# Expert results added to the residual in memory by the store; POOL's branches, its order and the zeroing moved

## The chip, the core and the metric

The kernel runs on one core of a Trainium2 chip. The metric is device microseconds of one execution. A core has a matrix engine (PE), a vector engine (DVE), an activation engine (ACT), a general engine (POOL, which also issues the indirect DMAs and writes their descriptors in software) and a queue engine (SP) that issues plain DMAs. All DMAs share 16 DMA engines. Times below are microseconds (us) from the start of the profiled span.

## What is computed

One layer of a diffusion backbone on 512 tokens of width 1024: a token mixer (state-space scan and convolution), then a mixture of 32 experts in 4 groups of 8. Every token chooses one group, and in it two experts. The part that the change touches:

```python
def hier_moe(h, w_rg, b_rg, w_rx, b_rx, w_gate, w_up, w_down):
    group_prob = softmax(h @ w_rg + b_rg)
    p_group, g_idx = top_k(group_prob, 1)
    top_logits, top_idx = top_k(in_group, 2)             # logits of the chosen group's 8 experts
    weights = softmax(top_logits) * p_group
    expert_id = g_idx * 8 + top_idx
    gate = sum(one_hot(expert_id, 32) * weights)
    for e in range(32):
        act = silu(h @ w_gate[e]) * (h @ w_up[e])        # 1024 -> 256
        out = out + gate[:, e:e + 1] * (act @ w_down[e]) # 256 -> 1024
...
x = x + gt2 * hier_moe(modulate(rmsnorm(x, g_ffn), sh2, sc2))
return rmsnorm(x, g_final)
```

Both experts of a token lie in one group, so experts of different groups never share a token. An expert's three weight matrices are 1 MB each, 3 MB together in float32.

## The kernel before

**Up to the experts.** The mixer takes the first 500 us or so. While its last product runs, `route(i)` (L1160) normalises one block of 128 tokens, stores it to the DRAM buffer `h2d`, and finds the block's two experts per token and each token's rank within its expert. The residual rows go to the DRAM buffer `x1d` (L1238). `indices` (L1279) then makes the table `ix` on DVE: for expert and slot, the token's row, twice over, as the first or the second choice of the token; empty slots get an index out of bounds, whose row the DMA leaves alone. `ixh` is the same for half rows.

**Preparation.** POOL zeroes five tiles (`xgs`, three of them, and `xws`, two, 128 x 1024 each) with memsets at L1260. `gather_e(e)` (L1423) fetches up to 64 token rows of an expert from `h2d` into half of an `xgs` tile: POOL loads the expert's size class from `size`, branches over four sizes and issues one indirect DMA of the chosen number of rows. `gather_w(e)` fetches rows 64 to 127 into `xws`, under a branch that is taken only for experts with more than 64 tokens (four experts are such here).

**The loop** at L1731 has 33 passes, step e for e = 0 to 32. The experts' order ORD is the 28 that aren't the last of their group, group by group, and then the four last ones of the groups (DIR), "expert e" being the e-th in this order. In step e PE runs gate and up of expert e (`tile_gu`, L1366: 8 slices of the inner dimension, two column halves each), then four small transposes of expert e-1's activated product (`tile_at`, tiles `sge`, `pat`, `at`; the two copies to `at` are on ACT and DVE), in odd steps the transposes (`turn`) of the next two experts' tokens, and down of expert e-1 (`tile_down`). `second` holds, under branches on PE, the same work for an expert's rows above 64. DVE then scales the result by gt2 into `ye` (`tile_y`), and POOL scatters it with indirect DMAs to `ybuf`, a DRAM buffer of 1024 rows, one for each token and choice (`scatter_e`; the second half again under a branch on size). The weights stream through 20 buffers of 1 MB: `load_p` of SP issues three loads at the end of each step, each as its buffer comes free; the last is number 95. PE, ACT and DVE follow the written order inside the loop (`MAN`, L1703); POOL and SP follow the framework's scheduler.

**ybuf** is zeroed early: POOL fills a tile, and four stores of 1 MB on ACT's queue (`y_zero`, 71 to 92 us) write it out.

**The end.** For tokens without an expert in DIR: SP loads x1 (`last_loads`) and both results of each token (`last_rows`, tile `yr`, after all scatters), ACT and DVE weight and add them (`last_scale`, `last_mix`), POOL adds the sum to x1 with a tensor operation (helper line L98), ACT sums squares (`last_sum`), and after `roots` and `recip` DVE scales (`last_out`) and POOL stores the rows. For tokens with an expert in DIR, the four last experts' rows are finished in place: POOL gathers x1's rows (`own_rows`, tile `ownb`), the token's weights from a small table (`lw` from `pwd`) and its other expert's result from `ybuf` (`own_other`, tile `owny`); DVE adds that (`own_base`) and the expert's own result (`own_sum`), and `own_out` stores the row. The routing weights come from `weights()` (L1266) and `last_tables()` (L1567), both called in step 1.

Where a wait is written with `<-`, the profile names the work that ended last before it; `PEq` is PE's own sequencer working through branches.

Of the kernel before, what the change touches and what calls it, by code (L numbers as in the profile page):

```python
# [26 lines left out]
def hybrid_kernel(  # L27
# [565 lines left out]

    ybuf = dram.tile([2 * L, D], F32, name="ybuf")
    zero = s5m.tile([64, TC, 128], F32, tag="ys", name="zero", bufs=1).rearrange("p t n -> p (t n)")
    G.memset(zero, 0.0)

    def y_zero(j):
        S.dma_start(out=ybuf.rearrange("(p a) d -> p a d", p=64)[:, 4 * j:4 * j + 4], in_=zero.unsqueeze(1).to_broadcast([64, 4, D]))

    MANM = {mybir.EngineType.PE, mybir.EngineType.Activation}
    with tc.manual_schedule(engines=MANM):
# [8 lines left out]
        for j in range(4):  # L611
            KO[f"y{j}"] = lambda j=j: y_zero(j)
# [12 lines left out]
        for o in (  # L625
# [7 lines left out]
        ).split():  # L633
            if o not in done:
                KO[o]()
                done.add(o)
# [327 lines left out]
    G.iota(posf[:, :, :, 1], pattern=[[1, NT], [NT, 2]], base=0, channel_multiplier=0, allow_small_or_imprecise_dtypes=True)  # L964
# [63 lines left out]
    ORD = [x_ for x_ in range(NE) if x_ not in DIR] + list(DIR)  # L1028
# [250 lines left out]
    def indices(pt, p, n, name):  # L1279

        em = mz2.tile([128, 2, n], F32, tag="ixe", name=name + "_e", bufs=1)[0:p]
        t = mz2.tile([128, 2, n], F32, tag="ixs", name=name + "_s", bufs=1)[0:p]
        V.tensor_copy(t, pt)
        V.tensor_scalar(em[:, 0], t[:, 0], 0.0, BIG, op0=ALU.is_equal, op1=ALU.mult)
        V.scalar_tensor_tensor(em[:, 1], t[:, 1], 128.0, t[:, 0], op0=ALU.mult, op1=ALU.add)
        V.scalar_tensor_tensor(em[:, 1], em[:, 0], -1.0, em[:, 1], op0=ALU.add, op1=ALU.add)
        ix = mz2.tile([p, 2, n], I32, tag="ix" + name, name=name)
        V.tensor_copy(ix[:, 1], em[:, 1])
        V.tensor_scalar(em[:, 0], em[:, 1], float(L), -float(L), op0=ALU.is_ge, op1=ALU.mult)
        V.tensor_tensor(ix[:, 0], em[:, 0], em[:, 1], op=ALU.add)  # L1290
        if name == "tb":

            pq = ps_tp("pixh")
            for a in range(2):
                for c in range(2):
                    T.matmul(pq[64 * c:64 * c + 64, n * a:n * a + n], lhsT=ident[:, 64 * a:64 * a + 64], rhs=em[:, 1], start=True, stop=True, skip_group_check=True)
            V.tensor_scalar(ixh.rearrange("p a e -> p (a e)"), pq[:, 0:2 * n], 2.0, cofs, op0=ALU.mult, op1=ALU.add)
        return ix

# [10 lines left out]
    V.tensor_copy(ixw, ix[64:128, 0])  # L1310
# [22 lines left out]
    V.tensor_scalar(s0[:, 1:1 + NE - ND].rearrange("p (g e) -> p g e", g=NGR), c64[:, :, 0:EPG - 1], 64.0, None, op0=ALU.is_gt)  # L1333
    V.tensor_scalar(s0[:, 1 + NE - ND:1 + NE], c64[:, :, EPG - 1], 64.0, None, op0=ALU.is_gt)
# [11 lines left out]
    def scatter(idx, y):  # L1346
        return G.indirect_dma_start(out=ybuf, out_offset=bass.IndirectOffsetOnAxis(ap=idx, axis=0), in_=y, in_offset=None,
                             bounds_check=2 * L - 1, oob_is_err=False)
# [17 lines left out]
    def tile_gu(pg, e, r, a):  # L1366
        st = (xws[e // 2 % 2] if a else xgs[e // 2 % 3]).rearrange("p (k s) -> p k s", k=KD)
        for k in range(KD):
# [29 lines left out]
    def tile_y(pd):  # L1398
# [8 lines left out]
    more = {}  # L1407

    def by_size(e, f, lo=0, hi=len(SIZES)):
        if hi - lo == 1:  # L1410
            return [f(SIZES[lo])]
        mid = (lo + hi) // 2
        with tc.If(more[e] > mid - 1) as big:
            r = by_size(e, f, mid, hi)
        with big.Else():
            r += by_size(e, f, lo, mid)
        return r
# [5 lines left out]
    def gather_e(e):  # L1423

        if e < NE:
            more[e] = load_size(e, EN.Pool)
            p0 = 64 * (e % 2)
            by_size(e, lambda n: gather(xgs[e // 2 % 3][p0:p0 + n], ix[0:n, 0, ORD[e]:ORD[e] + 1]), 0, SIZES.index(64) + 1)

    def gather_w(e):  # L1430

        if e < NE:
            p0 = 64 * (e % 2)
            with tc.If(more[e] > SIZES.index(64)):  # L1434
                gather(xws[e // 2 % 2][p0:p0 + 64], ixw[0:64, ORD[e]:ORD[e] + 1])

    scattered = []

    def scatter_h(e, a, y):
        return G.indirect_dma_start(out=ybuf.rearrange("r (c n) -> (r c) n", c=2), out_offset=bass.IndirectOffsetOnAxis(ap=ixh[:, a, ORD[e]:ORD[e] + 1], axis=0),  # L1440
                                    in_=y[:, 512 * a:512 * a + 512], in_offset=None, bounds_check=4 * L - 1, oob_is_err=False)

    def halves(size_, f):

        r = [f(0)]
        with tc.If(size_ > SIZES.index(64)):  # L1446
            r.append(f(1))
        return r

    def scatter_e(e, y):  # L1450
        ins = halves(more[e], lambda a: scatter_h(e, a, y))

        for i_ in ins:
            for p_ in scattered:
                tc.declare_no_dep(i_.ins if hasattr(i_, "ins") else i_, p_.ins if hasattr(p_, "ins") else p_, reason="rows of different experts")
        scattered.extend(ins)

    for e in range(4):
        gather_e(e)
    for e in range(3):  # L1460
        gather_w(e)
# [4 lines left out]
    with tc.If(n_gen > 0):  # L1466
        with tc.For_i(0, n_gen, 1):
# [17 lines left out]
            for i in range(NT):  # L1485
                for q in range(2):
# [5 lines left out]
                    rg = mz2.tile([128, 2], BF16, tag="rg", name="rg", bufs=2)  # L1492
                    V.tensor_scalar(rg, pos[:, i, q, :], g8[:, 0:1], None, op0=ALU.mult)
                    T.matmul(pt[:, 0:2], lhsT=og, rhs=rg, start=(n == 0), stop=(n == 2 * NT - 1))
                    n += 1
            ixg = indices(pt[:, 0:2].unsqueeze(2), 128, 1, "tg")
# [15 lines left out]
            gather(xg, ixg[:, 0])  # L1512
# [27 lines left out]
            for h in range(2):  # L1540
                V.tensor_tensor(yg[:, 512 * h:512 * h + 512], pd[h], gt2[:, 512 * h:512 * h + 512], op=ALU.mult)
            scattered.append(scatter(ixg[:, 1], yg))
# [4 lines left out]
    x1s, yrs, ids = [], [], {}  # L1547
# [3 lines left out]
    BC = (0, 1, 6, 7)  # L1551
    DC = (2, 4, 8, 10)

    def ins_of(i):
        return i.ins if hasattr(i, "ins") else i

    def after_all(ld):
        for p_ in scattered:
            tc.add_manual_dep(ins_of(ld), ins_of(p_).name, mybir.DependencyInfo(mybir.DependencyClass.Sync, mybir.DependencyReason.DATA), reason="results of every expert")

    def half_rows(t):
# [273 lines left out]
```

## Time and profile before

| | us |
|---|---|
| median of 3 runs | 904.88 (902.15 to 905.14) |
| the profiled execution, its own time | 905.64 |
| its span, first to last instruction | 903.9 |
| PE busy | 708.6 (78%) |
| DVE busy | 497.3 (55%) |
| POOL busy | 370.2 (41%) |
| ACT busy | 321.4 (36%) |
| DMA moved | 202.80 MB, mean 224 GB/s |
| mean granted TensorE clock | 0.91 of full speed |

The shares are means over stages with different limits. The experts' part lies between about 536 us and the end; the rows below are of that part, but for the software queue's, which is of the whole span. In a row of the timeline, the time in square brackets is how long the engine had been idle before the instruction, and what ended that.

### The profile page before, as it was taken

Reading aid. Unit: us, or ns where it says so; the run is one execution under the profiler, and the core shown is the slowest. Engines: PE = TensorE matmul, PEld = TensorE weight load, DVE = VectorE, ACT = ScalarE, POOL = GpSimd, SP = SyncE. Lnnn points to the kernel's source line nnn. Section 1 sums busy time; section 2 is a strip of 40 time slices with the busy share of each in tenths; the row PEclk is TensorE's granted clock in tenths of the full one; section 3 lists DMA queues with packets and bytes.
Section 4 is the critical chain, followed back from the end, with each engine's and each line's share of the span. In section 5 each row is a group of like instructions: output and inputs, shape, how many; then the busy total and the mean of one; then the engine's idle time right before and its main releaser. Section 6 shows DMA issues by size and latency. Waiting matters only on the chain. (4 is left out here: it accounts for less than half of the span.)

```text
span 903.9 us, 14338 instructions
## 1 busy us (share of the span) xinstructions
PE 708.6 (78%) x5334; PEld 484.4 (54%) x5334; DVE 497.3 (55%) x824; ACT 321.4 (36%) x564; POOL 370.2 (41%) x323
## 2 busy tenths in 40 slices
PE   3598967998969977889999963887988999994430
PEld 0476854666657765646788742454555455552200
DVE  4948573365489878538883584332233443430783
ACT  4443512346455747538432311311111121210350
POOL 4656434435386796613400232143132222344342
PEclk9998987999999998989999985897999999998655
DMA  8925951242246464667857385999999999998001
GB/s 308 256 77 161 234 177 53 72 123 71 66 135 193 147 184 139 194 207 287 309 199 274 117 309 167 378 353 344 331 384 367 384 382 380 384 398 323 18 38 56
DMA packets 87160, 202.80 MB, mean 224 GB/s; under 512 B 15025, under 2 KB 44787, under 8 KB 77346
## 3 DMA queue, kind: packets, MB, share of 16 engines
q1 hardware_dynamic: 77410, 177.92, 56.5%
q0 software_dynamic: 7680, 15.30, 5.0%
q10 hardware_dynamic: 1984, 8.44, 3.5%
q8 instruction: 54, 0.88, 0.4%
q14 instruction: 32, 0.26, 0.1%
HBM read 183.05 MB, written 27.23 MB: 233 GB/s over the span
## 5 line engine op out<-in xcount | busy, mean ns | idle before, releaser
L1370 PE MATMUL peg<-eraw,xg 128*64 128x256 f32 x1024 | 120.0, 386 | 8.8 <-PEq L1708 6.9
L1370 PEld LDWEIGHTS peg<-eraw,xg 128*64 128x64 f32 x1024 | 81.3, 139 | 54.7 <-issue 28.7
L1392 PE MATMUL ped<-eraw,at 128*64 128x512 f32 x288 | 77.4, 666 | 18.4 <-ACT at L1385 15.5
L396 PE MATMUL zp<-hh,zuwh 128*128 128x512 f32 x192 | 78.5, 409 | 0.0
L1440 POOL DMA_INDIRECT ybuf<-ye,ixh x31 | 31.2, 1007 | 113.0 <-DVE ye L1402 76.6
L398 PE MATMUL zp<-hh,zuwl 128*128 128x512 f32 x192 | 76.9, 400 | 0.3 <-POOL zuwl L757 0.2
L397 PE MATMUL zp<-hl,zuwh 128*128 128x512 f32 x192 | 76.6, 399 | 0.0
L98 POOL TENSOR_TENSOR adacc<-adacc,wa 128x512 f32<-128x512 f32 x30 | 46.6, 1553 | 42.5 <-ACT wa L857 40.1
L1402 DVE TENSOR_TENSOR ye<-ped,gt2h 128x512 f32<-128x512 f32 x56 | 36.3, 687 | 34.3 <-PE ped L1392 31.8
L1343 POOL DMA_INDIRECT xg<-h2d,tb x32 | 30.0, 937 | 57.0 <-ACT at L1385 33.0
L1385 ACT ACTIVATE at<-pat 128x128 f32<-128x128 f32 x32 | 8.8, 276 | 109.4 <-PE pat L1383 57.5
L1392 PEld LDWEIGHTS ped<-eraw,at 128*64 128x64 f32 x288 | 19.1, 147 | 50.2 <-issue 23.8
L396 PEld LDWEIGHTS zp<-hh,zuwh 128*128 128x128 f32 x192 | 37.2, 194 | 11.8 <-issue 4.4
L1383 PE MATMUL pat<-ident,sge 64*128 64x64 f32 x128 | 16.2, 309 | 34.2 <-DVE sge L1377 34.2
L398 PEld LDWEIGHTS zp<-hh,zuwl 128*128 128x128 f32 x192 | 37.0, 193 | 9.6 <-POOL zuwl L757 1.6
L1386 DVE COPY at<-pat 128x128 f32<-128x128 f32 x32 | 9.3, 292 | 59.0 <-PE pat L1383 48.9
L397 PEld LDWEIGHTS zp<-hl,zuwh 128*128 128x128 f32 x192 | 37.1, 193 | 7.3
L1359 DVE COPY xw<-pxt 128x512 f32<-128x512 f32 x16 | 11.1, 692 | 51.8 <-PE pxt L1354 34.8
L1383 PEld LDWEIGHTS pat<-ident,sge 64*128 64x128 f32 x128 | 11.0, 202 | 48.8 <-DVE sge L1377 36.7
L1377 DVE TENSOR_TENSOR sge<-peg,sge 64x256 f32<-64x256 f32 x64 | 27.4, 428 | 14.5 <-ACT sge L1375 12.7
L98 POOL TENSOR_TENSOR vb<-vta,vtb 128x512 f32<-128x512 f32 x16 | 21.9, 1370 | 30.8 <-PE pv L533 20.0
L1375 ACT ACTIVATE sge<-peg 64x512 f32<-64x512 f32 x32 | 18.9, 590 | 39.9 <-PEq L1708 28.5
(510 smaller groups left out, 1770.1 us busy)
## 6 DMA issues: line engine op xcount, KB each, us to landing
eraw<-in_w_exp_gate_dram SPq DMA_DIRECT2D x24, 1024.0 KB
eraw<-in_w_exp_up_dram SPq DMA_DIRECT2D x24, 1024.0 KB
eraw<-in_w_exp_down_dram SPq DMA_DIRECT2D x24, 1024.0 KB
wa<-in_w_ada_dram SPq DMA_DIRECT2D x32, 512.0 KB
zr<-in_w_in_dram SPq DMA_DIRECT2D x12, 1024.0 KB
wa<-in_w_ada_dram SPq DMA_DIRECT2D x8, 1024.0 KB
eraw<-in_w_exp_gate_dram SPq DMA_DIRECT2D x14, 512.0 KB
eraw<-in_w_exp_down_dram SPq DMA_DIRECT2D x14, 512.0 KB
```

The lines of the kernel that those rows point to most:

```text
L98: G.tensor_tensor(o, a, b, op=op)
L396: T.matmul(acc, lhsT=wh, rhs=ah, start=start, stop=False)
L397: T.matmul(acc, lhsT=wh, rhs=al, start=False, stop=False)
L398: T.matmul(acc, lhsT=wl, rhs=ah, start=False, stop=stop)
L1343: G.indirect_dma_start(out=xg, out_offset=None, in_=h2d, in_offset=bass.IndirectOffsetOnAxis(ap=idx, axis=0), bounds_check=L - 1, oob_is_e ...
L1370: T.matmul(pg[H[c], 256 * a:256 * a + 256], lhsT=st[:, k, H[e % 2]], rhs=r[c][k // 4][:, 256 * (k % 4):256 * (k % 4) + 256], start=(k == 0 ...
L1375: S.activation(sg[64:128], pg[0:64], AF.Silu)
L1377: V.tensor_tensor(sg[H[k], k:512:2], pg[64:128, k:512:2], sg[64:128, k:512:2], op=ALU.mult)
L1383: T.transpose(pas[k][:, 64 * a:64 * a + 64], sg[H[k], 256 * a + k:256 * a + 256:2], ident[H[k], H[k]])
L1392: T.matmul(pd[a][H[c]], lhsT=at[:, 128 * k + 64 * a:128 * k + 64 * a + 64], rhs=r[2][k][:, 512 * c:512 * c + 512], start=(k == 0), stop=(k ...
L1402: V.tensor_tensor(y[:, 512 * a:512 * a + 512], pd[a], gt2h, op=ALU.mult)
L1440: return G.indirect_dma_start(out=ybuf.rearrange("r (c n) -> (r c) n", c=2), out_offset=bass.IndirectOffsetOnAxis(ap=ixh[:, a, ORD[e]:ORD[ ...
```

## The change

- A result is weighted when it leaves PSUM: `slot_weights()`, new and called before the loop, brings each token's routing weight into the order of the expert's slots (`wh`, by matmuls with the one-hot matrix `oh`, in three bfloat16 parts), and `tile_y` multiplies by `wh` and gt2 in one DVE operation.
- `add_e` replaces `scatter_e`: two indirect DMAs per expert (both halves, always) that add the rows to `x1d` in memory (`compute_op=ALU.add`). `ybuf`, its zeroing, `pwd` and `last_tables` are gone. Adds of experts of one group wait for that group's earlier adds; those of other groups share no token and are declared independent.
- ORD takes the groups in turn: expert 0 of each group, then expert 1 of each, and so on. The last four are the same as before.
- POOL follows the written order in the loop, and `gather_e`, `gather_w`, the adds and the final stores are issued always, with no size load and no branch; the gather has always 64 rows.
- The zeroing of `xgs`, `xws`, the PSUM tiles and `ownb` is done by ACT (a copy with scale 0).
- `tile_gu` is split: 6 of 8 slices, then `tile_at`, then the last 2. The first `turn` of `xws` moves behind gu of expert 0.
- The end loads x1 with SP after all adds (`last_rows`, step 28), gathers `ownb` for group j after that group's adds (`own_rows`, one in each of steps 26 to 29), and has no mixing; `last_sum` runs in step 30, the first `roots` and `last_out` in step 31, the rest in step 32 and after it.

The diff, cut to its core:

```diff
-    def y_zero(j):
-        S.dma_start(out=ybuf.rearrange("(p a) d -> p a d", p=64)[:, 4 * j:4 * j + 4], in_=zero.unsqueeze(1).to_broadcast([64, 4, D]))
...
-    ORD = [x_ for x_ in range(NE) if x_ not in DIR] + list(DIR)
+    ORD = [EPG * g_ + i_ for i_ in range(EPG) for g_ in range(NGR)]
...
+    def zero(t):
+        n = t.shape[1] // 128
+        S.activation(t.rearrange("p (k n) -> p k n", k=n), ident.unsqueeze(1).to_broadcast([128, n, 128]), AF.Copy, scale=0.0)
+
     for a_ in xgs + xws:
-        G.memset(a_, 0.0)
+        zero(a_)
...
+    def add_rows(dst, idx, y, rows):
+        return G.indirect_dma_start(out=dst, out_offset=bass.IndirectOffsetOnAxis(ap=idx, axis=0), in_=y, in_offset=None,
+                                    bounds_check=rows - 1, oob_is_err=False, compute_op=ALU.add)
...
-            V.tensor_tensor(y[:, 512 * a:512 * a + 512], pd[a], gt2h, op=ALU.mult)
+            V.scalar_tensor_tensor(y[:, 512 * a:512 * a + 512], pd[a], wh[:, a, ORD[e]:ORD[e] + 1], gt2h, op0=ALU.mult, op1=ALU.mult)
...
     def gather_e(e):
         if e < NE:
-            more[e] = load_size(e, EN.Pool)
             p0 = 64 * (e % 2)
-            by_size(e, lambda n: gather(xgs[e // 2 % 3][p0:p0 + n], ix[0:n, 0, ORD[e]:ORD[e] + 1]), 0, SIZES.index(64) + 1)
+            gather(xgs[e // 2 % 3][p0:p0 + 64], ix[0:64, ORD[e]:ORD[e] + 1])
...
+    def add_e(e, y):
+        added[e] = [add_rows(half_rows(x1d), ixh[:, a, ORD[e]:ORD[e] + 1], y[:, 512 * a:512 * a + 512], 2 * L) for a in range(2)]
+        for n_, i_ in enumerate(added[e]):
+            for e_ in added:
+                for p_ in added[e_][:n_] if e_ == e else added[e_]:
+                    if e_ == e or ORD[e_] // EPG != ORD[e] // EPG:
+                        tc.declare_no_dep(ins_of(i_), ins_of(p_), reason="rows of different tokens")
+                    else:
+                        after(i_, [p_])
+
+    for f, e in ((gather_e, 0), (gather_e, 1), (gather_w, 0), (gather_w, 1), (gather_e, 2), (gather_e, 3), (gather_w, 2)):
+        f(e)
+    weights()
+    slot_weights()
...
     def own_rows(j):
-        own_get(half_rows(x1d), own["b"][j], 1, j, 2 * L)
-        own_get(pwd, own["w"][:, j], 0, j, 4 * L)
+        for a in range(2):
+            ld = G.indirect_dma_start(out=own["b"][j][:, a], out_offset=None, in_=half_rows(x1d),
+                                      in_offset=bass.IndirectOffsetOnAxis(ap=ixh[:, a, DIR[j]:DIR[j] + 1], axis=0), bounds_check=2 * L - 1, oob_is_err=False)
+            after(ld, further + [p_ for e in range(j, NE - ND, NGR) for p_ in added[e]])
...
     def last_rows():
-        for i in range(NT):
-            t = eraw("yr").rearrange("p (q d) -> p q d", q=2)
...
+        for h in range(2):
+            t = eraw("x1").rearrange("p (i d) -> p i d", i=2)
+            ld = SY.dma_start(out=t, in_=x1d[256 * h:256 * h + 256].rearrange("(i p) d -> p i d", p=128))
+            after(ld, further + [p_ for e in added for p_ in added[e]])
+            x1s.extend([t[:, 0], t[:, 1]])
...
-    MAN = {EN.PE, EN.Activation, EN.DVE}
+    MAN = {EN.PE, EN.Activation, EN.DVE, EN.Pool}
...
         for e in range(NE + 1):
+            n_ = e - 1 - NE + ND
             gather_e(e + 4)
             if e > 0:
                 sg = tile_act(pgs[(e - 1) % 2])
+            if e == NE:
+                for i in (2, 3):
+                    last_out(i)
+                own_out(0)
+            if e == NE - 2:
+                for i in (0, 1):
+                    last_sum(i)
+            if e == NE - 1:
+                roots(0)
+                recip(0)
+                for i in (0, 1):
+                    last_out(i)
             if e < NE:
-                tile_gu(pgs[e % 2], e, eraws[e], 0)
+                tile_gu(pgs[e % 2], e, eraws[e], 0, range(0, 6))
             if e > 0:
                 at = tile_at(sg)
+            if e < NE:
+                tile_gu(pgs[e % 2], e, eraws[e], 0, range(6, KD))
...
             if 0 < e <= NE - ND:
-                scatter_e(e - 1, tile_y(pd))
+                add_e(e - 1, tile_y(e - 1, pd))
             if e > NE - ND:
-                if e < NE:
-                    own_base(e - 1 - NE + ND)
-                own_sum(e - 1 - NE + ND, pd)
+                own_sum(n_, pd)
+                own_add(n_)
             gather_w(e + 3)
...
-            if e == 1:
-                weights()
-                last_tables()
             if e == NE - 6:
                 last_loads()
+            if NE - 6 <= e < NE - 2:
+                own_rows(e - NE + 6)
             if e == NE - 4:
                 last_rows()
```

## Rows read from the trace of the kernel before

**Rows 1.** Busy time by stretch: PE, PEld, DVE, ACT, POOL, PEclk, DMA share, GB/s.

```profile
718.00:797.00 79.00, 72.24 (x534) 43.98 (x533) 34.02 (x66) 15.79 (x33) 21.78 (x23) 1.00 1.02 379
...
822.00:845.00 23.00, 3.10 (x27) 1.76 (x24) 4.98 (x8) 3.06 (x6) 9.83 (x9) 0.66 0.63 230
```

**Rows 2.** Timeline of PE over two steps: start, duration, engine, line, tiles.

```profile
778.30 3.67 PE L1370 MATMUL peg<-eraw,xg 128*64 128x256 f32 x32 [0.31 <-PEq L1708]
...
790.24 1.94 PE L1392 MATMUL ped<-eraw,at 128*64 128x512 f32 x8 [0.41 <-ACT at L1385]
...
792.49 3.67 PE L1370 MATMUL peg<-eraw,xg 128*64 128x256 f32 x32 [0.31 <-PEq L1708]
```

**Rows 3.** Busy time by stretch of 10 us, about the last weights' landing.

```profile
805.00:815.00 10.00, 9.28 (x68) 5.22 (x64) 3.42 (x7) 1.74 (x4) 6.65 (x5) 1.00 1.01 414
815.00:825.00 10.00, 8.79 (x74) 5.83 (x72) 0.69 (x1) 0.60 (x1) 1.03 (x1) 1.00 0.78 268
```

**Rows 4.** Timeline of the end, from the last weight's issue on.

```profile
801.96 0.33 SPq L1021 DMA_DIRECT2D eraw<-in_w_exp_down_dram  x1
...
813.84 1.03 POOL L1440 DMA_INDIRECT ybuf<-ye,ixh  x1 [0.30 <-issue]
...
821.38 2.27 SPq L1684 DMA_DIRECT2D yr<-ybuf  x4
...
838.40 1.42 DVE L1637 SCALAR_TENSOR_TENSOR ownb<-owny,lw,ownb 128x512 f32<-128x512 f32 x2 [16.55 <-DMA ownb<-x1d,lix]
...
844.46 0.38 PE L1383 MATMUL pat<-ident,sge 64*128 64x64 f32 x1 [19.74 <-DVE sge L1377]
...
846.38 5.44 PE L1392 MATMUL ped<-eraw,at 128*64 128x512 f32 x16 [0.89 <-ACT at L1385]
...
852.25 3.67 PE L1370 MATMUL peg<-eraw,xg 128*64 128x256 f32 x32 [0.44 <-PEq L1711]
```

**Rows 5.** Timeline from the zeroing to the loop's first gate and up.

```profile
536.60 4.67 DVE L1176 TENSOR_SCALAR rsc<-io,rsc 128x4 f32<-128x4 f32 x1
536.70 2.75 POOL L1260 MEMSET xg<- 128x1024 f32 x3
...
542.39 0.21 DVE L1176 TENSOR_SCALAR rsc<-io,rsc 128x4 f32<-128x4 f32 x1
...
547.42 0.16 DVE L1288 CAST tb<-tb_e 128x32 int32<-128x32 f32 x1
...
549.45 1.00 POOL L1343 DMA_INDIRECT xg<-h2d,tb  x1 [8.21 <-DVE some L1337]
...
551.38 0.92 POOL L1343 DMA_INDIRECT xg<-h2d,tb  x1 [0.93 <-issue]
...
561.71 1.94 PE L1354 MATMUL pxt<-ident,xw 128*128 128x128 f32 x8 [2.06 <-issue]
563.58 5.19 PE L1370 MATMUL peg<-eraw,xg 128*64 128x256 f32 x32
```

**Rows 6.** Timeline of two early waits of PE, and POOL's table gathers.

```profile
583.25 0.33 PE L1383 MATMUL pat<-ident,sge 64*128 64x64 f32 x1 [3.02 <-DVE sge L1377]
...
602.41 1.00 POOL L1608 DMA_INDIRECT lw<-pwd,lix  x1 [0.30 <-issue]
...
613.14 3.68 PE L1392 MATMUL ped<-eraw,at 128*64 128x512 f32 x8 [5.69 <-ACT at L1385]
```

**Rows 7.** The scatters' line by itself: duration in ns, first and last start; landing.

```profile
L1440 POOL DMA_INDIRECT ybuf<-ye,ixh x31: 980/999/1034, 578.0 to 813.8; - x31
...
DMA to landing us min/median/max: 7.1/7.1/7.1
```

**Rows 8.** The page's DMA queues: packets, MB, share of 16 engines' span.

```profile
q0 software_dynamic: 7680, 15.30, 5.0%
```

**Rows 9.** Timeline: prices of an ACT and of a DVE pass.

```profile
859.42 1.04 ACT L1696 ACTIVATE yr<-eraw 128x1024 f32<-128x1024 f32 x1
...
881.25 0.75 DVE L1642 SCALAR_TENSOR_TENSOR owny<-ped,lw,gt2h 128x512 f32<-128x512 f32 x1 [1.36 <-issue]
```

More of the change, by code (lines that the diff above doesn't have):

```diff
@@ L1364, in hybrid_kernel, with tile_gu @@
     H = [slice(64 * c, 64 * c + 64) for c in range(2)]
-    def tile_gu(pg, e, r, a):
+    def tile_gu(pg, e, r, a, ks):
         st = (xws[e // 2 % 2] if a else xgs[e // 2 % 3]).rearrange("p (k s) -> p k s", k=KD)
-        for k in range(KD):
+        for k in ks:
             for c in range(2):
@@ L1433, in gather_w, with ins_of, after @@
             p0 = 64 * (e % 2)
[L1434 to L1461, printed above, removed]
+            gather(xws[e // 2 % 2][p0:p0 + 64], ixw[0:64, ORD[e]:ORD[e] + 1])
+    added, further = {}, []
+    def ins_of(i):
+        return i.ins if hasattr(i, "ins") else i
+    def after(i_, ps_):
+        for p_ in ps_:
+            tc.add_manual_dep(ins_of(i_), ins_of(p_).name, mybir.DependencyInfo(mybir.DependencyClass.Sync, mybir.DependencyReason.DATA), reason="sums of the same rows")
+    def add_e(e, y):
[11 more added lines that the diff above has]
+    slot_weights()
     itr = mz2.tile([1, 4], F32, name="itr")
@@ L1511, in hybrid_kernel @@
             G.memset(xg, 0.0)
-            gather(xg, ixg[:, 0])
+            gather(xg, ixg)
             xt_ = new_y()
@@ L1549, in hybrid_kernel @@
     ssf = mz2.tile([128, 2, 12], F32, name="ssf")
     GRP = ((0, 6), (6, 10), (10, 12))
[L1551 to L1561, printed above, removed]
-        return t.rearrange("r (c n) -> (r c) n", c=2)
@@ L1595, in last_loads @@
+    BC = 0
+    DC = (4, 6, 8, 10)
     def last_loads():
-        for h in range(2):
-            t = eraw("x1").rearrange("p (i d) -> p i d", i=2)
-            SY.dma_start(out=t, in_=x1d[256 * h:256 * h + 256].rearrange("(i p) d -> p i d", p=128))
-            x1s.extend([t[:, 0], t[:, 1]])
         t = eraw("gfin")
@@ L1624, in own_rows @@
-    def own_rows(j):
-        own_get(half_rows(x1d), own["b"][j], 1, j, 2 * L)
-        own_get(pwd, own["w"][:, j], 0, j, 4 * L)
-    def own_other(j):
-        for ld in own_get(half_rows(ybuf), own["y"][j], 2, j, 4 * L):
-            after_all(ld)
-    def own_base(j):
+        own["b"], own["y"] = [], []
+        for i in range(2):
+            t = eraw("ownb")
+            zero(t)
+            v = t.rearrange("p (j a n) -> p j a n", j=2, a=2)
+            own["b"] += [v[:, 0], v[:, 1]]
+    def own_rows(j):
+        for a in range(2):
+            ld = G.indirect_dma_start(out=own["b"][j][:, a], out_offset=None, in_=half_rows(x1d),
+                                      in_offset=bass.IndirectOffsetOnAxis(ap=ixh[:, a, DIR[j]:DIR[j] + 1], axis=0), bounds_check=2 * L - 1, oob_is_err=False)
+            after(ld, further + [p_ for e in range(j, NE - ND, NGR) for p_ in added[e]])
+            for e in added:
+                if e % NGR != j:
+                    for p_ in added[e]:
+                        tc.declare_no_dep(ins_of(ld), ins_of(p_), reason="rows of different tokens")
+            own.setdefault("ld", []).append((j, ld))
@@ L1666, in no_order @@
                 tc.declare_no_dep(ins_of(i_), ins_of(p_), reason="rows of different tokens")
-        stored.extend(ins)
+            stored.append(i_)
     def own_out(j):
@@ L1722, in hybrid_kernel @@
         for t in pgs + pd:
-            V.memset(t, 0.0)
-        for xs_ in (xgs, xws):
-            turn(xs_[0], pts)
-            turned(xs_[0], pts)
+            zero(t)
+        turn(xgs[0], pts)
+        turned(xgs[0], pts)
         for m in range(13, 17):
@@ L1747, in hybrid_kernel @@
                     last_out(i)
-                for j in (0, 1):
-                    own_out(j)
+            if e < NE:
+                tile_gu(pgs[e % 2], e, eraws[e], 0, range(0, 6))
             if e > 0:
                 at = tile_at(sg)
-            if e == NE - 1:
-                roots(0)
-                last_sum(2)
+            if e < NE:
+                tile_gu(pgs[e % 2], e, eraws[e], 0, range(6, KD))
+            if e == NE - 2:
+                for i in (2, 3):
+                    last_sum(i)
             if e == NE:
-                last_sum(3)
                 roots(1)
+                recip(1)
+                own_out(1)
             nxt = e % 2 == 1 and e + 2 < NE
             p_ = (e + 1) // 2
+            if e == 0:
+                turn(xws[0], pts)
+                turned(xws[0], pts)
             if nxt:
```

205 lines of the change are left out of this document (80 added, 125 removed), and 6 rows, old and new, of the table w1.

## The prediction

> **What bounds the kernel now.** I read first the busy table by stretch, then the chain at the end, then the loop's own steps, then its start.
>
> The change touches only the experts' part, from about 536 us. Step e below is one pass of the loop at L1731; it multiplies gate and up (gu) of the e-th expert in the kernel's order and down of the one before.
>
> Middle of the loop: the DMA engines are saturated (share 1.02 at 379 GB/s from 718 to 797) while PE is busy 72.24 of 79 us [rows 1]. Two steps take 792.49 - 778.30 = 14.19 us, 7.1 each, in which PE's own work leaves only gaps of 0.3 to 0.4 [rows 2]. PE paces the steps, and the DMA keeps just ahead.
>
> End of the loop: here the time goes. The last expert weight is issued at 801.96 [rows 4], the DMA is full until 815 and slackens after it (share 1.01, then 0.78) [rows 3]: all weights are there at about 815. Yet gu of step 31 starts only at 852.25 [rows 4], and the span ends at 903.9. Between them PE does 3.10 us of work in 23 us [rows 1]: the step before waits 19.74 us for sge, sge stands behind a DVE operation that waited 16.55 us for gathered rows (ownb), and those and the loads of yr stand behind the last scatters, since POOL issued the last at 813.84 and SP the loads at 821.38 [rows 4]. From 852.25 to 903.9, 51.7 us, DVE and ACT run a chain of sums, roots and stores.
>
> Start: POOL zeroes five tiles from 536.70, and a DVE operation of 4 elements a partition that starts at 536.60 lasts 4.67 us; the index chain follows it to the first gather (549.45) and gu of step 0 (563.58) [rows 5].
>
> **The change part by part.**
>
> *Zeroing on ACT.* POOL's memsets go (three take 2.75 us), and I take the 4.67 us of the DVE operation as held by them: the next one of its line takes 0.21 [rows 5]. Gain 4.5 us, on the path. ACT's five zero fills cost about 1.04 each, the price of an ACT pass over 1024 columns [rows 9], 5.2 us in a stretch where ACT waits for PE anyway; without that cover the first fill, 1.0 us, would be late. PSUM's four fills move from DVE to ACT, hidden in the same wait.
>
> *Gathers without branches, fewer index operations.* The index cast is ready at 547.42, the first gather starts at 549.45 because it also waits for the sizes, and the second comes 1.93 later; unbranched ones follow each other by 1.00 + 0.30 [rows 6]. The second gather so ends 2 us earlier. The turn of xw (561.71, 1.94 us) leaves the path before gu of step 0 [rows 5]. Against that stand weights() and slot_weights(), now ahead of the loop: some 25 small DVE operations of 0.2 us, 12 small matmuls and one ACT Exp, 8 to 10 us beside the first gathers' flight (a scatter lands after 7.1 us, [rows 7]); I let 1 us stick out, bounds 0 and 4. Sum: 4.5 + 2 + 1.9 - 1 = about 7 us: gu of step 0 at 556.5 and the weights' loads about as much earlier. Gathers and second halves that are now issued always cost POOL 1.0 to 1.3 us each, four per step, 5.2 of 7.1 us: no bound. Rows out of bounds I take to move nothing: the software queue's 15.30 MB [rows 8] are about what valid rows make (4.2 gathered, 3.7 scattered, 4.2 stored as x1d and h2d, some 3 at the end).
>
> *Weights out of step 1.* PE waited 3.02 us there for sge behind weights() and last_tables(), and 5.69 us at 613.14 for a chain that began with late gathers behind five table gathers on POOL [rows 6]. Both go: 8.7 us of PE's time.
>
> *Split of gu into 6 and 2 parts.* The wait of 0.41 us for at [rows 2] gets the last quarter of gu as cover; in odd steps the turn covered it already. 16 x 0.41 = 6.6 us of PE's time. The scalar multiply by slot weight makes each half of DVE's ye cost 0.75 [rows 9], under 0.1 more; DVE is busy 34 of 79 us [rows 1].
>
> PE alone would so reach step 31 about 7 + 8.7 + 6.6 = 22 us earlier, plus the stall of 20. But the weights must be there.
>
> *Scatters become adds into x1d.* The old value of each row must be read as well as written. The kernel before scatters 28 of 32 experts: 1024 x 4 KB x 28/32 = 3.67 MB. The software queue moved 15.30 MB in 5.0% of 903.9 us, 2.95 us per MB [rows 8]. One more pass is 10.8 us of full DMA. Bounds: 0 (the loop's DMA absorbs it, as it does the plain scatter) and 12 (all of it, and some). Weights then are complete between 815 - 7 = 808 and 820; I take 814, the middle, since table gathers and their 8-byte rows leave the same queues. By the plain scatter's row alone it would be 808, and the end some 6 us earlier. The Trainium skill, "Collectives: The Full Stack", section "The bandwidth ceiling: the fold count and why AG ≠ RS ≠ AR", says that an add in the DMA costs no cycles but reads two sources, and so runs at half a copy's rate: an estimate from it is the whole 10.8 us, weights at 819, the end some 5 us later. No row here shows an add.
>
> Each add waits for its group's earlier adds, four steps back, about 30 us; at a landing of 7.1 us [rows 7] none waits. Queued behind a waiting add on POOL: gathers for three steps ahead.
>
> *Zeroing ybuf early, 4 MB in all.* It goes from a stretch where PE is the bound; I put it at 0 (0 to 2).
>
> *The end.* Gone: yr's loads and scaling, the other results' gathers, POOL's adds. New: SP's two x1 loads wait for every add, and ACT's last_sum, in step 30, waits for them ahead of the copy at that PE needs. By weights at 814 and about 3 us for each 1 MB load, expert 29's are there 7 loads earlier, 793. Its step sees ye of expert 27 at 794.5; POOL, which has waited in own_rows(1) for the adds of expert 25 (issued at about 782) until 792 and then issued its two gathers, is free at about 795 and issues two adds by 797.6; landing 7.1 (as a store) to 14 (twice), I take 10: 807.6. The two loads stand behind the weights: first megabyte at 814 + 3 = 817, with latency 818. Two last_sums of 1.04 and their read-outs: 820.5. at, then both halves of down, 5.44 us [rows 4], as expert 29 keeps its second half: 826.3. That is gu of step 31: **826 instead of 852.25**.
>
> From there to the end, 51.7 us before: POOL's two slow adds leave, roots(0), two last_outs (2.5 us) and own_out(0) move ahead of at on DVE, two store issues of 1.3 us are added after the last root, as both halves are always stored. Net -1 us, 50.5. Span 826 + 50.5 = 876.5 instead of 903.9. The profiled run's own time lay 1.74 above its span and 0.76 above the median of the runs, so the forecast in the median's terms is 876.5 + 1.74 - 0.76 = **877.5 us**, 27 below 904.88.
>
> **The rivals.**
>
> *A, more is gained.* Adds land like stores and weights are done at 808: x1 arrives before ACT wants it, PE sets step 31 at about 815: 866 us. For it: PE's ideal, and landing 7.1. Against: the DMA's share of 1.02.
>
> *B, adds are late but within four steps.* POOL is in fixed order, and own_rows(0) and (1) wait for adds 24 and 25 ahead of adds 26 and 27. With a landing of 20 us instead of 10, add 25, issued at 782, lands at 802; own_rows(1) lets add 27 go at 805 to 807.6, it lands at 828, the first megabyte of x1 at 832, the sums end at 834.5, down at 840, and the end comes 50.5 later: 890.5 of span, 891.5 us. At 24 us of landing it is 8 more: 899.5, and no gain left to measure soon after.
>
> *C, slower.* An add that lands later than four steps (some 30 us) blocks POOL in each round: 6 rounds times (L - 30), plus L - 10 at the end. It eats the 27 us from L = 31 us on; at 34 it gives 877 + 24 + 24 = 925. For it: DMA share 1.02 beside reads and writes of HBM. Against: 7.1 us for the scatter in that same crowd.
>
> *D, POOL becomes the bound.* Four indirect DMAs a step instead of two to four, and DVE holds POOL while it writes their descriptors: if each waited out one DVE pass of 0.75 us [rows 9], a step would be 4 x 2.05 = 8.2 us instead of 7.1, and 32 steps give 877 + 35 = 912; it decides from 0.5 us a DMA on. Against it: the 31 scatters took 980 to 1034 ns each [rows 7], beside a DVE busy 34.02 of 79 us [rows 1]. The Trainium skill, "SBUF — State Buffer", section "A bandwidth-pool intuition that's wrong (but worth ruling out)", tells of such a lock by certain DVE copies, with a DMA lengthened five times; by that rule D would hold and be dearer, but the scatters' durations show no sign of it.
>
> *E, the change doesn't do what it says at the start:* the DVE operation was not held by the memsets; then 4.5 us of the gain are missing: 882, inside the range.
>
> **How the numbers follow.** Forecast with E: 0.55, 868 to 888. A: 0.17, 857 to 868. B: 0.14 for 888 to 902, and 0.05 for 902 to 907.5. C 0.07, D 0.02. A measurement tells about 0.3%, 2.7 us, from no change. Faster (below 902.2): 0.55 + 0.17 + 0.14 = 0.86; within: 0.05; slower: 0.07 + 0.02 = 0.09. Range, with A's lower end and most of B: 857 to 896.
>
> **What would show it.** Start: no DVE operation over 1 us at the zero fills; gu of step 0 near 556. Loop: no wait for at of 0.41 in even steps; DMA share still near 1. End: ACT waiting some 10 us in step 30 for x1, step 31 near 826, then 50 us. Wrong if adds land past 14 us, if POOL waits for an add in mid-loop, or if PE waits for weights before step 28.

## The result

The changed kernel takes **950.24 us** (median of 4 runs, 947.86 to 953.74) against 903.51 for the kernel before on the same chip: ratio **1.053**, 95% interval 1.048 to 1.058. The forecast was 877.5, range 857 to 896: wrong in sign and by 73 us. The profiled execution has a span of 952.0 and an own time of 953.74.

**The start went as forecast.** The timeline answers to [rows 5]:

```profile
537.18 0.22 DVE L1166 TENSOR_SCALAR rsc<-io,rsc 128x4 f32<-128x4 f32 x1
...
544.68 1.04 POOL L1378 DMA_INDIRECT xg<-h2d,tb  x1 [8.12 <-DVE ixw L1346]
546.03 1.19 POOL L1378 DMA_INDIRECT xg<-h2d,tb  x1 [0.30 <-issue]
...
556.80 5.71 PE L1409 MATMUL peg<-eraw,xg 128*64 128x256 f32 x32 [2.98 <-issue]
```

From the DVE operation to gu of step 0 pass 19.62 us; before it was 563.58 - 536.60 = 26.98. The long DVE operation is gone, 0.22 for 4.67.

**The loop lost the time.** Busy time over the stretch of [rows 1], with the same columns:

```profile
718.00:797.00 79.00, 60.49 (x374) 32.42 (x376) 23.86 (x45) 10.52 (x22) 40.52 (x32) 0.85 0.88 307
```

PE falls from 72.24 busy us to 60.49, its granted clock from 1.00 to 0.85 of full speed, and the DMA, full before, to 0.88. Nothing there is a bound, so something waits. The waits of 560 to 860 us (engine, tile, line, what ended the wait: us in total, times, longest) name it, and the timeline of two steps shows it:

```profile
ACT xw L1397 <- DMA xw<-h2d,ixw: 60.5, 8, 10.5
DVE xw L1398 <- DMA xw<-h2d,ixw: 59.8, 8, 10.4
PE pat L1422 <- DVE sge L1416: 47.6, 18, 8.6
```

```profile
694.67 0.60 ACT L1397 ACTIVATE xw<-pxt 128x512 f32<-128x512 f32 x1 [7.07 <-DMA xw<-h2d,ixw]
...
702.41 1.41 DVE L1441 SCALAR_TENSOR_TENSOR ye<-ped,wh,gt2h 128x512 f32<-128x512 f32 x2 [3.73 <-PE ped L1431]
...
703.44 1.57 POOL L1386 DMA_INDIRECT x1d<-ye,ixh  x1 [0.96 <-DVE ye L1441]
...
705.32 1.56 POOL L1386 DMA_INDIRECT x1d<-ye,ixh  x1 [0.31 <-issue]
...
707.18 0.99 POOL L1378 DMA_INDIRECT xw<-h2d,ixw  x1 [0.30 <-issue]
...
715.81 0.60 ACT L1397 ACTIVATE xw<-pxt 128x512 f32<-128x512 f32 x1 [7.20 <-DMA xw<-h2d,ixw]
...
716.43 0.59 ACT L1414 ACTIVATE sge<-peg 64x512 f32<-64x512 f32 x1
716.54 1.41 DVE L1441 SCALAR_TENSOR_TENSOR ye<-ped,wh,gt2h 128x512 f32<-128x512 f32 x2
...
718.46 0.38 PE L1422 MATMUL pat<-ident,sge 64*128 64x64 f32 x1 [5.36 <-DVE sge L1416]
```

In every odd step ACT and DVE copy the turned `xw`, whether or not an expert has rows there. `xw` is now fetched for every expert. The second fetch of a pair stands on POOL behind two adds of the even step: `ye` at 702.41, adds at 703.44 and 705.32, the fetch at 707.18, the copy that its landing releases at 715.81. Behind the waiting copies stand the silu and `ye`, and behind those PE's transposes. A pair of steps takes 715.81 - 694.67 = 21.1 us here, against 14.19 [rows 2].

**The end** answers to [rows 4]: last add, x1's loads, gu of step 31, last store.

```profile
893.12 1.56 POOL L1386 DMA_INDIRECT x1d<-ye,ixh  x1 [0.30 <-issue]
...
896.24 0.90 SPq L1656 DMA_DIRECT2D x<-x1d  x2
...
911.99 2.81 PE L1409 MATMUL peg<-eraw,xg 128*64 128x256 f32 x24 [0.43 <-PEq L1677]
...
946.41 0.99 POOL L1649 DMA_INDIRECT out_dram<-ownb,ixh  x1 [0.30 <-issue]
```

From gu of step 31 to the end of the span 40.0 us pass, against 51.7 before. The loss so lies wholly between step 0 and step 31: 911.99 - 556.80 = 355.2 us, where before had 288.7 and the forecast 269.5.

### The profile page after: what moved, and what is told of

It is laid out like the page before. It is cut to its first block, busy times and chain, and to the rows that moved or that the text cites. A ratio compares the mean times of both kernels' runs of the same rounds, so it can differ in the third digit from the quotient of the medians.

```text
span 952.0 us, 14158 instructions
## 1 busy us (share of the span) xinstructions
PE 734.4 (77%) x5350; PEld 490.9 (52%) x5350; DVE 475.9 (50%) x807; ACT 326.6 (34%) x570; POOL 427.9 (45%) x357
## 3 DMA queue, kind: packets, MB, share of 16 engines
q0 software_dynamic: 16384, 14.83, 6.4%
HBM read 189.60 MB, written 30.36 MB: 231 GB/s over the span
## 5 line engine op out<-in xcount | busy, mean ns | idle before, releaser
L1386 POOL DMA_INDIRECT x1d<-ye,ixh x56 | 88.3, 1576 | 175.4 <-DVE ye L1441 162.9
L1409 PE MATMUL peg<-eraw,xg 128*64 128x256 f32 x1024 | 138.7, 417 | 12.2 <-PEq L1674 7.1
L1431 PE MATMUL ped<-eraw,at 128*64 128x512 f32 x288 | 80.3, 686 | 4.3 <-DVE at L1425 3.1
L1398 DVE COPY xw<-pxt 128x512 f32<-128x512 f32 x16 | 11.1, 692 | 131.7 <-PE pxt L1393 65.0
L1441 DVE SCALAR_TENSOR_TENSOR ye<-ped,wh,gt2h 128x512 f32<-128x512 f32 x56 | 39.8, 747 | 53.1 <-PE ped L1431 50.2
L1422 PE MATMUL pat<-ident,sge 64*128 64x64 f32 x128 | 19.8, 320 | 59.6 <-DVE sge L1416 59.6
L1397 ACT ACTIVATE xw<-pxt 128x512 f32<-128x512 f32 x16 | 9.6, 597 | 133.1 <-PE pxt L1393 65.6
L1431 PEld LDWEIGHTS ped<-eraw,at 128*64 128x64 f32 x288 | 22.0, 158 | 40.6 <-issue 30.0
L1378 POOL DMA_INDIRECT xw<-h2d,ixw x32 | 31.6, 988 | 9.8 <-issue 9.1
```

The costliest lines, as they stand in the source:

```text
L1378: G.indirect_dma_start(out=xg, out_offset=None, in_=h2d, in_offset=bass.IndirectOffsetOnAxis(ap=idx, axis=0), bounds_check=L - 1, oob_is_e ...
L1386: return G.indirect_dma_start(out=dst, out_offset=bass.IndirectOffsetOnAxis(ap=idx, axis=0), in_=y, in_offset=None, bounds_check=rows - 1, ...
L1398: V.tensor_copy(xg[:, 512:1024], pts[1])
L1409: T.matmul(pg[H[c], 256 * a:256 * a + 256], lhsT=st[:, k, H[e % 2]], rhs=r[c][k // 4][:, 256 * (k % 4):256 * (k % 4) + 256], start=(k == 0 ...
L1422: T.transpose(pas[k][:, 64 * a:64 * a + 64], sg[H[k], 256 * a + k:256 * a + 256:2], ident[H[k], H[k]])
L1431: T.matmul(pd[a][H[c]], lhsT=at[:, 128 * k + 64 * a:128 * k + 64 * a + 64], rhs=r[2][k][:, 512 * c:512 * c + 512], start=(k == 0), stop=(k ...
```

## Experiments

Two theories. **W**: the fetch of second halves, issued for every expert and placed behind the adds, is waited for. **A**: the adds in memory are themselves the loss (1.57 us each on POOL where the scatter took 1.00 [rows 7], later landing, more traffic). All ratios are to the kernel before on the same chip. Its medians were 900.93 us beside experiments 1 to 4, 900.10 beside 5 to 8 and 903.60 beside 9 and 10, so a difference of times between these groups is good to 3 or 4 us; there the ratios decide.

**1. Second halves fetched by size again.**

```diff
-            gather(xws[e // 2 % 2][p0:p0 + 64], ixw[0:64, ORD[e]:ORD[e] + 1])
+            with tc.If(load_size(e, EN.Pool) > SIZES.index(64)):
+                gather(xws[e // 2 % 2][p0:p0 + 64], ixw[0:64, ORD[e]:ORD[e] + 1])
```

> The changed kernel, but the second half of an expert's rows (gather_w) is again fetched only where the expert has more than 64 tokens, under a branch of POOL on the size, as in the kernel before. Theory W (in every odd step ACT and DVE copy the turned xw, and that copy waits for the second halves' gather, which is now issued for every expert, behind two adds of 1.57 us, one step ahead): 28 of 32 waits go, a step takes about 7.1 us again, and with the 40 us that follow gu of step 31 in the changed kernel the time is 860 to 890 us. Rival A (the adds in memory are the loss: 1.57 us on POOL, more traffic, later landing): adds stay, so 930 to 950 us.

Measured: 893.08 us, ratio 0.992 (0.989 to 0.994). W's direction, a little slower than its range: the few fetches that remain are still late, PE waits for them three times, 23.8 us in all.

**2. Both fetches of a pair issued early, no branch.**

```diff
-    for f, e in (..., (gather_w, 2)):
+    for f, e in (..., (gather_w, 2), (gather_w, 3)):
...
+            if e % 2 == 1:
+                gather_w(e + 3)
+                gather_w(e + 4)
             if 0 < e <= NE - ND:
                 add_e(e - 1, tile_y(e - 1, pd))
...
-            gather_w(e + 3)
```

> The changed kernel with every second half still fetched, without a branch, but both gathers of a pair of experts issued at the end of the odd step before, ahead of that step's adds, one for each of the four that the loop now has in odd and even steps. Their landing of 8.6 us then lies beside a whole even step. Theory W: 860 to 890 us, like the kernel with the branch. Rival A (adds): 930 to 950 us.

Measured: 884.88 us, ratio 0.982 (0.979 to 0.985): 65 us less than the changed kernel, with the same instructions and the same bytes, only in another order on POOL. No wait for `xw`'s fetch is left in the loop. What is late next is an add: DVE may not write `ye` before the add of two steps earlier has read it.

```profile
DVE ye L1441 <- DMA x1d<-ye,ixh: 42.8, 12, 6.1
```

```profile
DMA to landing us min/median/max: 2.9/12.0/19.4
```

The first line is from the waits, the second from the instructions of the adds' line, where the landing is given for those that something waited for.

**3. Plain stores in place of the adds (sums left out).** `compute_op=ALU.add` is removed from `add_rows`.

> The changed kernel with plain stores in the place of the adds, in the same order and with the same waits: the sums are left out, so the output lacks all results but the last stored of each row. Theory W: the gather that ACT and DVE wait for is issued 2 x 0.57 us earlier in each pair of steps, 14 pairs, some 16 us: 925 to 945 us. Rival A: the adds' price goes: under 890 us.

Measured: 913.15 us, ratio 1.013 (1.009 to 1.016). Between the theories: 37 us less than the changed kernel, twice what W gave for it. ACT still waits for `xw`'s fetch (44.4 us in 8 times, 60.5 with adds), and in all 15 odd steps together it waits 95.7 us before its copy of `xw` where it waited 126.2 with adds; these 30.5 us answer to most of the 37. An add ahead of the fetch so costs more than its 0.57 us on POOL, the only term in W's 16 us; how much of the rest is its later landing wasn't told apart. A store takes POOL 1.01 us, an add 1.57, from the instructions of the line in this kernel, then in the changed one (ns, least, median, most):

```profile
L1386 POOL DMA_INDIRECT x1d<-ye,ixh x56: 1002/1014/1038, 572.6 to 852.9; - x56
```

```profile
L1386 POOL DMA_INDIRECT x1d<-ye,ixh x56: 1561/1573/1637, 578.9 to 893.1; - x56
```

**4. The kernel before, second halves fetched for every expert.**

```diff
-            with tc.If(more[e] > SIZES.index(64)):
-                gather(xws[e // 2 % 2][p0:p0 + 64], ixw[0:64, ORD[e]:ORD[e] + 1])
+            gather(xws[e // 2 % 2][p0:p0 + 64], ixw[0:64, ORD[e]:ORD[e] + 1])
```

> The kernel before with one edit: second halves are fetched for every expert, without the branch. Theory W: from ye of an even step to the turn of xw there are about 8.5 us, against a scatter's 1.0, the gather's 1.0 and a landing of 8.8: a wait of 2 to 3 us in each of 15 pairs, and more where PE loses clock: 930 to 965 us, with ACT and DVE waiting for xw in most odd steps. Rival A: 28 more gathers of no rows cost nothing, 900 to 910 us.

Measured: 900.97 us, ratio 0.999 (0.997 to 1.002). W, as stated there, is refuted: fetching always costs this kernel nothing. The timeline of POOL shows why: its order is the scheduler's, which puts both fetches of a pair around the odd step's scatter, a step ahead of the even step's.

```profile
661.61 0.95 POOL L1343 DMA_INDIRECT xw<-h2d,ixw  x1 [2.59 <-issue]
664.02 1.02 POOL L1439 DMA_INDIRECT ybuf<-ye,ixh  x1 [1.46 <-DVE ye L1402]
665.34 0.96 POOL L1343 DMA_INDIRECT xw<-h2d,ixw  x1 [0.31 <-issue]
672.59 1.01 POOL L1439 DMA_INDIRECT ybuf<-ye,ixh  x1 [6.29 <-issue]
```

So W is narrowed: it takes the fetch for every expert **and** POOL's written order, which has the second fetch behind the even step's adds.

**5. The changed kernel, POOL in the scheduler's order.** `EN.Pool` is taken out of `MAN`.

> The changed kernel with one edit: POOL's instructions of the loop are put in order by the planner again, as in the kernel before, not in the order of the program. The kernel before with empty second fetches (900.97 us, no loss) showed that the planner issues both gathers of a pair around the odd step's scatter, a step ahead of the place where the program has the second. Theory W (the hand's order puts that gather behind two adds of the even step, and ACT's and DVE's copy of xw waits for its landing): the planner takes it ahead, 880 to 895 us. Rival A (the adds' own price): 930 to 950 us.

Measured: 891.64 us, ratio 0.992 (0.989 to 0.994): the narrowed W holds. Some waits of ACT for `xw`'s fetch stay (27.1 us in 5 times), which the early order of experiment 2 hasn't.

**6. Early fetches and plain stores (sums left out).** Experiments 2 and 3 together.

> The kernel with the pair's gathers issued early (884.88 us), with plain stores in the place of the adds: the sums are left out. It measures the add's price where nothing else waits: the software queue took 6.6% of 883 us there and 5.1% of 912 with plain stores, some 12 us less of full DMA, and the landing falls from 12.0 to about 7 us, so that DVE no longer waits for the ye buffer (42.8 us in 12 waits). If adds cost time on the path: 865 to 876 us. If their price is hidden: 880 to 886 us.

Measured: 878.19 us, ratio 0.976 (0.974 to 0.979). Under the hidden case and a little above the other: 6.7 us less than experiment 2, some 5 by the two ratios. That is the adds' whole price here, with POOL's 0.57 us each, their traffic and DVE's wait for the `ye` buffer, which is gone with stores. The four kernels in one table (us):

| | second fetch behind the adds | both fetches early |
|---|---|---|
| adds | 950.24 | 884.88 |
| plain stores | 913.15 | 878.19 |

The adds cost 37 us where their 1.57 us and their traffic lie ahead of a fetch that is waited for, and 5 to 7 where no fetch is waited for.

**7. Early fetches, and the second add only where an expert has more than 64 tokens.**

```diff
-        added[e] = [add_rows(...) for a in range(2)]
+        added[e] = [half(0)]
+        with tc.If(load_size(e, EN.Pool) > SIZES.index(64)):
+            added[e].append(half(1))
```

> The kernel with the pair's gathers issued early (884.88 us), and the second add of an expert (the rows past its 64th) only where it has more than 64 tokens, under a branch of POOL: 28 adds of no rows less, 28 x 1.87 = 52 us of POOL, 7.34 MB less of writes by the memory's counter. If the empty adds lengthen the landing of the others and DVE's wait for the ye buffer: 872 to 880 us. If the loop is bound by DMA bytes and the end by PE: 881 to 887 us.

Measured: 874.55 us, ratio 0.971 (0.968 to 0.975). 25 adds without a row are left out, not 28, as three of the 28 experts have more than 64 tokens (31 of 56 adds remain): 10 us less. In the waits DVE's wait for `ye`'s add is gone. Now the end reads as the prediction told it, with an addition:

```profile
812.10 1.63 POOL L1386 DMA_INDIRECT x1d<-ye,ixh  x1 [7.82 <-DMA ownb<-x1d,ixh]
...
820.94 0.90 SPq L1661 DMA_DIRECT2D x<-x1d  x2
...
825.81 1.06 ACT L1666 ACTIVATE xg<-x 128x1024 f32<-128x1024 f32 x1 [6.01 <-DMA x<-x1d]
...
834.36 2.81 PE L1409 MATMUL peg<-eraw,xg 128*64 128x256 f32 x24 [0.44 <-PEq L1682]
```

The add of expert 27 waits for the landing of `own_rows`' gathers, which read rows of other tokens: no code declares them independent.

**8. The same, second fetches by size too.** The edit of experiment 1 on experiment 7.

> The same with the second halves' gathers too only where an expert has more than 64 tokens: 28 gathers less, 7.34 MB less read by the memory's counter. If reads of rows that go nowhere cost DMA time: 3 to 10 us under the run without this edit. If they only cost POOL's 1.0 us each: the same within 2 us; if the branches hold POOL back, as in the kernel with the branch at the old place (893 us): slower by up to 8 us.

Measured: 876.90 us, ratio 0.975 (0.973 to 0.978). That is 2.4 us more than the run without it, and no run of the one is as fast as the slowest of the other: leaving out 28 gathers without a row gains nothing once they are early. The edit also brings back 32 branches of POOL, so what the gathers alone cost isn't shown.

**9. Adds of the last experts declared independent of the other groups' `own_rows`.**

```diff
+            for j_, ld_ in own.get("ld", []):
+                if j_ != ORD[e] // EPG:
+                    tc.declare_no_dep(ins_of(i_), ins_of(ld_), reason="rows of different tokens")
```

> The kernel with early gathers and one add for small experts (874.55 us), and the last adds no longer ordered behind the landing of own_rows' gathers, which read rows of other groups' tokens (in that kernel the add of expert 27 waits 7.82 us for the landing of rows of ownb, SP's loads of x1 follow it, and ACT waits 6.0 us for x1 in step 30, ahead of the copy that PE needs). If that chain sets step 31: x1 is there some 7 us earlier, ACT's wait goes, 867 to 870 us. If the loads are late for another reason (the DMA's own work until 815): 873 to 876 us.

Measured: 875.37 us, ratio 0.970 (0.968 to 0.972); 874.55 without the edit, at a ratio of 0.971. The wait goes, the time stays:

```profile
799.76 1.63 POOL L1386 DMA_INDIRECT x1d<-ye,ixh  x1 [0.30 <-issue]
...
810.78 1.62 SPq L1664 DMA_DIRECT2D x<-x1d  x2
...
825.83 1.06 ACT L1669 ACTIVATE xg<-x 128x1024 f32<-128x1024 f32 x1 [9.93 <-DMA x<-x1d]
```

The loads are issued 10 us earlier and land at the same time. The DMA was full for some 9 of the 15 us that they took, up to about 820, and not after; busy time by stretches of 4 us, columns as in [rows 3]:

```profile
812.00:816.00 4.00, 1.90 (x18) 1.00 (x14) 2.60 (x5) 1.92 (x5) 0.93 (x1) 1.00 1.02 318
816.00:820.00 4.00, 1.93 (x12) 0.99 (x12) 1.08 (x3) 0.00 (x0) 0.00 (x0) 0.76 0.89 310
820.00:824.00 4.00, 0.00 (x0) 0.00 (x0) 0.00 (x0) 0.00 (x0) 0.00 (x0) 0.50 0.36 139
```

What held the loads in the last 6 us isn't shown.

**10. The copies that PE's down waits for ahead of x1's sums and the first outputs.** In step 30 all four `last_sum` stand behind `tile_at`, in step 31 `roots(0)`, `recip(0)` and two `last_out` too.

> The same, and in steps 30 and 31 the copies that PE's down waits for stand ahead of the sums of x1, the first roots and the first two outputs on ACT and DVE (the DVE copy of at stood behind two outputs of 1.24 us each, and PE's second half of down 2.9 us behind its first). If these stand on the path to the last store: 3 to 6 us under the run without this edit, 862 to 867 us. If DVE's own sums are later by as much: within 1.5 us of it.

Measured: 869.72 us, ratio **0.963** (0.961 to 0.966), the fastest version: 5.6 us under experiment 9, as expected, and 34 under the kernel before. The expected time itself, 862 to 867 us, was missed, as it counted on the gain that experiment 9 didn't bring. PE no longer waits for x1 in step 30:

```profile
820.12 0.28 ACT L1424 ACTIVATE at<-pat 128x128 f32<-128x128 f32 x1 [1.49 <-PE pat L1422]
...
826.69 2.81 PE L1409 MATMUL peg<-eraw,xg 128*64 128x256 f32 x24 [0.43 <-PEq L1685]
826.90 1.06 ACT L1669 ACTIVATE xg<-x 128x1024 f32<-128x1024 f32 x1 [6.50 <-DMA x<-x1d]
```

## Why the prediction was wrong

**The step that failed** is one sentence of the part on gathers without branches: "Gathers and second halves that are now issued always cost POOL 1.0 to 1.3 us each, four per step, 5.2 of 7.1 us: no bound." POOL indeed was no bound (40.52 of 79 us). But the sentence prices the issue and not the landing. It doesn't ask who waits for the fetched tile (ACT and DVE, in every odd step), nor what POOL's new written order puts ahead of the fetch. The rows needed were there: the one landing in [rows 7] took 7.1 us, as long as a step, and the second fetch is issued one step before its use. Experiments 2, 4 and 5 show it: order alone is worth 65 us in the changed kernel, and fetching always costs nothing in the kernel before. The adds belong to this as what stands ahead of the fetch: with plain stores in the same order 37 us of the loss go (experiment 3).

**The rivals** of the prediction. None of them was this. A and B set the end by the adds' landing; the changed kernel lost its time before the end, and x1's loads followed the last add there after 3.1 us. C (adds that land after four steps) didn't occur: POOL waited for no earlier add in the loop. D (POOL held while it writes descriptors) isn't seen either: an add takes POOL 1.57 us, steadily (1.56 to 1.64), and with only `compute_op` removed the same DMA takes 1.01 (1.00 to 1.04, experiment 3), so the longer time is the add's own price. E is refuted by the 0.22 us of the DVE operation. The 0.09 for slower was the sum of mechanisms that the rows spoke against; the one that decided had no chance of its own, and no sign of being wrong in the prediction's list names a wait for a fetch.

**The other terms**, read where the loop isn't held up:

- *Start*: 7 us forecast; 26.98 - 19.62 = 7.4.
- *The adds' traffic*: 10.8 us of full DMA forecast, bounds 0 and 12. The software queue took 6.6% of 883.4 us in experiment 2 and 5.2% of 876.2 with plain stores: 58.3 - 45.6 = 12.7, to within about 1 us by the rounding of the shares. The forecast let 6 us of it delay the end; stores instead of adds gave 5 to 7 us (experiment 6), but that holds DVE's wait for `ye` too, which the forecast hadn't, so the agreement may be luck. The Trainium skill's "Collectives: The Full Stack", section "The bandwidth ceiling: the fold count and why AG ≠ RS ≠ AR", says of reduce-scatter that its add reads two sources and so runs at about half of a copy's rate. The prediction's estimate from that and [rows 8], 10.8 us of the queue, agrees in size with these 12.7.
- *The adds' landing*: 10 us forecast; 12.0 in the median of those in experiment 2 that something waited for, up to 19.4. The 7.1 us that it started from is a single value: least, median and most in [rows 7] are equal. The part on adds asked who waits for an add and named POOL only; DVE, which has two `ye` buffers, waits too (42.8 us in experiment 2).
- *Empty DMAs*: "Rows out of bounds I take to move nothing" holds for the queue's bytes (14.83 MB), not for its packets (3600 fewer without 25 empty adds) or POOL's time: leaving these out gave 10 us.
- *Weights out of step 1 and the split of gu*: 8.7 and 6.6 us of PE's time forecast. PE's waits before down were 18.4 us in all before and 4.3 in experiment 2. As the next paragraph shows, the loop was no shorter for it.
- *The end*: x1 was forecast at 818 and step 31 at 826; in experiments 7 and 9 ACT got x1 at 825.8 and step 31 began at 834. In 7 the loads were issued late (820.94) and landed after 4.9 us; in 9 they were issued at 810.78 and took 15 us, 9 of them beside a full DMA, where the forecast had 4 from the last weight on. The rest from step 31 was forecast at 50.5 us and took 40.0 in the changed kernel: 11.7 us less than before, not 1. Of this 7.6 lie behind the last store's issue (13.2 us from there to the span's end before, 5.6 after). Little of that is data in flight: in the kernel before the DMA moves nothing from 895 on, and both spans last until a DRAIN instruction of POOL's queue at the end of the program has run, from 894.5 for 8.64 us before and from 944.0 for 7.16 us in the changed kernel (durations in ns, then first and last start):

```profile
895.00:900.00 5.00, 0.00 (x0) 0.00 (x0) 0.00 (x0) 0.00 (x0) 0.00 (x0) 0.50 0.00 0
...
L1830 POOLq DRAIN  x3: 46/99/8644, 894.5 to 903.7; - x3
```

```profile
L1788 POOLq DRAIN  x3: 46/105/7158, 944.0 to 951.7; - x3
```

Why it starts 3.8 us behind the last store's issue before, and 2.4 us ahead of it in the changed kernel, wasn't tried.

**That the sum came near in the end is luck.** Experiment 2, which differs from the changed kernel in POOL's order alone, and experiment 7, which also leaves the empty adds out, lie with 885 and 875 us in the range about 877.5. But from gu of step 0 to gu of step 31 the forecast had 269.5 us, and experiment 2 took 291.0, more than the 288.7 of before; experiment 7 took 834.36 - 552.52 = 281.8. In experiment 2 step 0 came 4.1 us sooner than forecast and the rest from step 31 was 10.5 us shorter, which covers 14.6 of the 21.5 us missed. Against the kernel before it gained 11.1 us up to step 0 and 11.7 from step 31 on; the loop gave nothing. Busy time of that stretch before, in the changed kernel and in experiment 2, columns as in [rows 1]:

```profile
563.58:852.25 288.67, 236.58 (x1689) 139.02 (x1689) 106.59 (x213) 52.02 (x101) 87.58 (x82) 0.94 0.94 346
```

```profile
556.80:911.99 355.19, 262.52 (x1697) 145.53 (x1697) 99.44 (x184) 55.22 (x106) 150.20 (x119) 0.87 0.80 273
```

```profile
552.44:843.42 290.98, 250.83 (x1696) 140.74 (x1697) 99.38 (x184) 55.23 (x106) 150.65 (x121) 0.94 0.96 335
```

These rows also tell the wait from the clock. The changed kernel takes 64.2 us more than experiment 2 here: PE is busy 11.7 us longer, at a mean granted clock of 0.87 against 0.94, and idle 52.5 us longer.

**What stays open**: in experiment 2 PE idles 12 us less in that stretch than before but is busy 14 us longer at the same mean clock of 0.94, and no run tells why. What held x1's loads after 820 in experiment 9, and what shortened the tail behind the last store, isn't explained.

## What to carry to other kernels

Where a branch that skipped a transfer is removed, price its landing and not only its issue: find who reads the tile unconditionally, what is queued behind that reader, and how long before it the transfer now stands in its queue's order. An engine that passes from a scheduler's order to a written one loses the early issues that the scheduler had found and the written order doesn't repeat, so list its instructions per step in the trace of before and write them in that order. In these runs transfers without a single valid row could stay where they were early (experiment 8), and those that others queue behind were worth a branch (experiment 7).

## What the runs showed of the hardware

An indirect DMA that adds takes POOL 1.57 us for 128 rows of 2 KB, the same DMA as a store 1.01. It makes 64 packets more: the software queue of the changed kernel, then of experiment 3 (packets, MB, share of 16 engines' span), 3584 packets more for 56 adds.

```profile
q0 software_dynamic: 16384, 14.83, 6.4%
```

```profile
q0 software_dynamic: 12800, 14.81, 5.1%
```

The memory's own counter shows no second read for an add (189.60 MB read, 30.36 written, with adds and with stores alike), though the queue's packets took 12.7 us more; where an add's second read goes isn't shown. The counter does take in rows that are out of bounds: experiment 4 reads 190.39 MB against 183.05, and 7.34 MB is 28 gathers x 64 rows x 4 KB, although these rows are all empty; experiment 7 writes 23.81 MB against 30.36, and 6.55 MB is 25 adds x 128 rows x 2 KB. In the queue's bytes neither shows, and 28 such gathers cost 80 packets each (9920 against 7680 [rows 8]).

A fetch by POOL that carries no valid row still takes a landing before its reader may go on: 715.81 - 707.18 = 8.6 us in the changed kernel, from its start on POOL to the copy that it releases, behind two adds in the same queue and beside full DMA engines (share 1.02 over these 8.6 us). The Trainium skill, "DMA: Bandwidth & Descriptors", section "Anatomy of one DMA — SWDGE (gpsimd) path", gives a fit per DMA of this path of 2.0 us and a microsecond for each 436 KB; an estimate from it for 64 rows of 4 KB is 2.6 us. The trace differs, and decides here; no run shows such a fetch alone, so the fit itself isn't tested.
